# Two decoder layers in split fp32: attention turns, mixes and gates set in another order, output projections opened by half slabs

## The chip, the core and the metric

The kernel runs on one core of a Trainium2 chip. Its engines are TensorE (PE, matrix products; PEld is its weight load, which the profile lists apart), VectorE (DVE), ScalarE (ACT), GpSimd (POOL) and the DMA queues, here issued by SyncE (SP). The metric is the device time of one execution in microseconds, the median of several runs.

## The reference

One sequence of 256 positions, width 2048, passes two pre-norm layers and a final norm, all in fp32. Layer 0 is latent attention with 16 heads (rank 512 for queries and for keys and values, 128 plain and 64 rotary dimensions a head, values of 128). Layer 1 is attention in a sliding window of 128 with 32 query heads and 4 key and value heads of 64, a learned sink a head, and rotation of the first 16 dimensions.

```python
def reference(x, positions, layer_norm, mla_w_in, mla_q_norm, mla_w_uq, mla_kv_norm,
              mla_w_ukv, mla_w_out, swa_w_in, swa_sinks, swa_w_out, final_norm):
    for i in range(DEPTH):
        h = rmsnorm(x, layer_norm[i])
        j = i // N_MIXERS
        if i % N_MIXERS == 0:
            y, gate = mla_mixer(h, positions, mla_w_in[j], mla_q_norm[j], mla_w_uq[j],
                                mla_kv_norm[j], mla_w_ukv[j])
            w_out = mla_w_out[j]
        else:
            y, gate = swa_mixer(h, positions, swa_w_in[j], swa_sinks[j])
            w_out = swa_w_out[j]
        x = x + (y * jax.nn.silu(gate)) @ w_out
    return rmsnorm(x, final_norm)

def mla_mixer(h, positions, w_in, q_norm, w_uq, kv_norm, w_ukv):
    ...
    q = (rmsnorm(c_q, q_norm) @ w_uq).reshape(B, S, MLA_HEADS, MLA_NOPE + MLA_ROPE)
    q_nope = q[..., :MLA_NOPE]
    q_rope = rope(q[..., MLA_NOPE:], positions, MLA_ROPE)
    kv = (rmsnorm(c_kv, kv_norm) @ w_ukv).reshape(B, S, MLA_HEADS, MLA_NOPE + MLA_V)
    k_nope, v = kv[..., :MLA_NOPE], kv[..., MLA_NOPE:]
    k_rope = rope(k_rope[:, :, None, :], positions, MLA_ROPE)[:, :, 0, :]
    y = mla_causal_attention(q_nope, q_rope, k_nope, k_rope, v)
    return y, gate

def swa_sink_attention(q, k, v, sinks):
    ...
    m = jnp.maximum(jnp.max(s, axis=-1, keepdims=True), sink)
    e = jnp.exp(s - m)
    p = e / (jnp.sum(e, axis=-1, keepdims=True) + jnp.exp(sink - m))
    o = jnp.einsum('bnhgqk,bnkhd->bnqhgd', p.astype(v.dtype), vw)
    return o.reshape(B, S, SWA_WIDTH)
```

## The kernel before

Everything is kept transposed: the width lies on the 128 partitions in 16 chunks, the 256 positions along the free axis. An fp32 product is made of three float32r matmuls, high times high, high times low and low times high (`proj`, L250 to L252). `slab` does eight chunks of that: 24 matmuls of 128x256, half of the sum over the width, so two slabs make one chunk of a projection.

**Weights.** They stream once from memory. `Weights` holds a list of pieces of up to 128x1024 in the order in which `w.add` names them; SP's queue loads them as `wraw` (512 KB each), ACT casts the high part `whi` (L89) and DVE subtracts to get the low part `wlo` (L90), two pieces ahead of the one in use, and loads run three further ahead. So the order of `w.add` has to be the order of use, and with it goes the order of work on SP, ACT and DVE.

**Layer 0.** After the latent projections (`cq`, `ck`, in `lat`) a loop over eight groups g of two heads runs on TensorE: plain queries from `cq` (24 matmuls), the mix of the group before, rope parts of the queries (12), keys from `ck` (24), values (24, L520 to L522: here `ck` is the stationary side and the weights move), then four gate slabs from `hs` (96). After the first slab come the scores (16), and after the third the turn: six transposes (`turn`, L342 and L343) that bring the softmax rows `p` under the keys. ACT and DVE make of them the high part `pth`, the low part `ptl`, and for the second half of the queries a plain fp32 tile `pt1`. The mix multiplies values by them (L450 to L453); L453 is a plain fp32 product, which TensorE runs as two passes, the others are float32r. Its result is multiplied by the gate (`sg`) and split into `ys`. The last mix stands alone in front of the output projection, 16 chunks of two slabs from `ys` (`w_o0`).

**Layer 1.** Two chunks of keys (four slabs each two), the sum of squares `total` (L222, plain fp32) after the first of them, `rsqrt` (DVE and POOL) to `r1`, its row `r1B`, the rotated keys `k1s`; then values from four quarters of the weights (`sc<-whi,hs`, L603 to L605). A loop over 16 pairs of query heads c follows, in which every step is a half query slab, values and gate of pair c-1 (`values`, `gated`), the turn of pair c, the scores of pair c+1, the other half of a query two pairs ahead, and a whole gate chunk. `silu` (L361 to L363) reads the gate's PSUM bank as `hx`. The second output projection (`w_o1`) and the tail with the final norm end the program.

**What sets the order.** Each engine runs its instructions in one fixed order; the framework derives it from the order of the calls and from its own priorities, so places differ a little from the code. `ps_p` has three PSUM banks for projections, `ps_s` two for scores, `ps_t` one tile for turns, `ps_y` one bank for mixes and values. `pth`, `ptl` and the value tiles have one buffer each.

Of the kernel before, what the change touches and what calls it, by code (L numbers as in the profile page):

```python
# [25 lines left out]
P = 128  # L26
# [17 lines left out]
WARM = 2  # L44
MASK_MLA = [(i + 16) % 32 for i in range(32)]
# [54 lines left out]
def trunk(ctx: ExitStack, tc: tile.TileContext, a: dict):  # L100
# [11 lines left out]
    w = Weights(nc, wpool, raw_bufs=5, sub_bufs=4, ahead_load=3, ahead_split=2)  # L112
    w.add(a["w_c"][0], SUB, SUB // 2)
# [8 lines left out]
    for c in range(KC):  # L122
        w.add(a["w_o0"][c], D)
# [6 lines left out]
    for c in range(KC):  # L130
        if c + 2 < KC:
            w.add(a["w_q1"][c + 2], D)
        w.add(a["w_g1"][c], D)
    for c in range(KC):
        w.add(a["w_o1"][c], D)
# [125 lines left out]

    def bank(pool_, tag):
        return pool_.tile([P, 512], F32, tag=tag, name=tag)
# [72 lines left out]
    def turn(pair, both):  # L336
# [9 lines left out]
        hi = work.tile([P, 6 * P], F32R, tag="pth", name="pth", bufs=1)  # L346
        lo = work.tile([P, 6 * P], F32R, tag="ptl", name="ptl", bufs=1)
# [20 lines left out]
    lat = {n: [const.tile([P, 2, S], F32R, tag=f"lat{n}{c}", name=f"c{n}{c}") for c in range(RC)] for n in "qk"}  # L368
# [73 lines left out]
    def mix(g, vt, pt, sgs):  # L442

        (vh, vl, v1), (pth, ptl, pt1) = vt, pt
        yp = bank(ps_y, "yp")
        for j in range(2):
            v = slice(j * VD, (j + 1) * VD)
            n = slice(j * S, (j + 1) * S)
            o = yp[:, n]
            mm(o, lhsT=vh[:, v], rhs=pth[:, n], start=True, stop=False)  # L450
            mm(o, lhsT=vl[:, v], rhs=pth[:, n], start=False, stop=False)
            mm(o, lhsT=vh[:, v], rhs=ptl[:, n], start=False, stop=False)
            mm(o[:, P:], lhsT=v1[:, v], rhs=pt1[:, j * P:(j + 1) * P], start=False, stop=True)  # L453
# [6 lines left out]
    mixes = None  # L460
    for g in range(HEADS // 2):
# [10 lines left out]
        if mixes:  # L472
            mixes()
        ps = bank(ps_p, "pp")[:, 0:S]
        up(ps, *w.next(), lat["q"])
        qr = work.tile([P, S], F32, tag="ro3", name="ro3")
        rope(qr, ps, cos0, sin0, MASK_MLA)
        qs = work.tile([P, 2, S], F32R, tag="qs", name="qs")
        stack_pair(qs, qr)
        if g == 0:  # L480
            t = bank(ps_y, "yp")
            tot = [q.total(t[:, 4 * i:4 * i + 4]) for i, q in enumerate((sq_x, sq_c["q"], sq_c["k"]))]
            r0 = rsqrt("r0", tot[0], D)

            sqc = rsqrt("sqc", tot[1], RANK, r0)
            nsq = const.tile([P, 2], F32, name="nsq")
            dve.tensor_tensor(out=nsq, in0=sqc, in1=r0, op=ALU.mult)
            dve.tensor_scalar(out=nsq, in0=nsq, scalar1=-MLA_SCALE, scalar2=None, op0=ALU.mult)
            skc = rsqrt("skc", tot[2], RANK, r0)
            sk = const.tile([P, 2], F32, name="sk")  # L490
            dve.tensor_tensor(out=sk, in0=skc, in1=r0, op=ALU.mult)
            t = bank(ps_y, "yp")
            r0B = row("r0B", r0, t[:, 0:S])
            skB = row("skB", sk, t[:, S:])
            ps = bank(ps_s, "sc")[:, 0:S]
            mm(ps, lhsT=fold, rhs=krn, start=True, stop=True)
            kr = work.tile([P, S], F32, tag="ro3", name="ro3")
            rope(kr, ps, cos0, sin0, MASK_MLA)
            dve.tensor_tensor(out=kr, in0=kr, in1=r0B, op=ALU.mult)
            split(krs, kr)  # L500
# [31 lines left out]
        for step in range(4):  # L532
# [24 lines left out]
            if step == 2:  # L557
                pth, ptl, pt1 = turn(pair, False)
# [359 lines left out]
```

## Time and profile before

| | us |
|---|---|
| runs | 681.96, 682.65, 677.71 |
| median | 681.96 |
| profiled execution, its own time | 679.97 |
| its span, first to last instruction | 678.2 |

The span and the time of the same execution differ by 1.77 us. The granted clock of TensorE is 0.999 over the span. The profile gives for each engine the busy time, and by windows of the span the busy time and the number of instructions in them; the timeline lists instructions with start and duration, and with the wait before them where there was one. The duration of a matmul (some 276 ns) is longer than its distance to the next one, since they are pipelined: the distance of the starts is what counts.

### The profile page before, as it was taken

The page shows a single profiled execution, that of the slowest core. Times are in us where ns is not written, and L with a number is a line of the kernel's source. Part 1 is how long each engine was busy: PE and PEld are TensorE (multiplying, and loading weights), DVE is VectorE, ACT ScalarE, POOL GpSimd, SP SyncE. Part 2 cuts the span into 40 slices and gives each one's busy share as a digit, 9 for nine tenths or more (in the row PEclk, how much of TensorE's full clock was granted, in tenths as well). Part 3 has the DMA queues.
Part 4 walks back from the last instruction along what each step waited for, and adds up shares of the span by engine and source line. Part 5 has one row for each costly group of instructions (what it writes and reads, how often), then busy time and mean ns, then how long its engine had stood idle before and what let it go on. Part 6 is the DMA issues. An engine that isn't in the chain of part 4 may idle for free.

```text
span 678.2 us, 14573 instructions
## 1 busy us (share of the span) xinstructions
PE 666.0 (98%) x5732; PEld 662.6 (98%) x5732; DVE 529.0 (78%) x1079; ACT 429.8 (63%) x855; POOL 66.4 (10%) x72
## 2 busy tenths in 40 slices
PE   8999999999999999999999999999999999999995
PEld 8899999999999999999999999999999999999995
DVE  4897886787787686666667799899899899766664
ACT  6666756756666675444445588878878878644431
POOL 3634000000000000111120000000000000022220
PEclk9999999999999999999999999999999999999999
DMA  8665344544554545555554554554553544565513
GB/s 310 236 221 176 137 162 170 174 155 147 179 172 141 183 160 182 185 192 181 189 183 163 169 175 143 169 187 128 184 183 130 186 167 145 162 208 191 191 59 125
DMA packets 34197, 116.99 MB, mean 173 GB/s; under 512 B 4177, under 2 KB 4817, under 8 KB 34129
## 3 DMA queue, kind: packets, MB, share of 16 engines
q1 hardware_dynamic: 33840, 115.54, 50.4%
q8 instruction: 45, 0.74, 0.4%
q10 hardware_dynamic: 288, 0.52, 0.2%
q14 instruction: 24, 0.19, 0.1%
HBM read 113.95 MB, written 2.10 MB: 171 GB/s over the span
## 4 chain that ended last, share of the span: by engine, by line
PE 90%; DVE 3%; ACT 3%; issue 1%; POOL 1%; DMA 1%; SPq 0%; DVEq 0%; ACTq 0%; POOLq 0%
PE pp L251 24%; PE pp L252 24%; PE pp L250 24%; ACT whi L89 2%; PE pt L342 2%; DVE wlo L90 1%; PE pp L748 1%; PE pp L520 1%; PE pp L522 1%; PE pp L521 1%; PE yp L670 1%; DMA wraw<-in_w_c 1%; PE pt L343 1%; PE sc L642 1%; PE sc L605 1%
## 5 line engine op out<-in xcount | busy, mean ns | idle before, releaser
L90 DVE TENSOR_TENSOR wlo<-wraw,whi 128x1024 fp32r<-128x1024 f32 (+1 forms) x217 | 259.6, 1198 | 96.1 <-ACT whi L89 96.0
L89 ACT CAST whi<-wraw 128x1024 fp32r<-128x1024 f32 (+1 forms) x217 | 222.7, 1028 | 135.5 <-PE pp L251 110.0
L252 PE MATMUL pp<-hs,wlo 128*128 128x256 f32 x860 | 237.9, 277 | 1.4 <-DVE wlo L90 1.4
L250 PE MATMUL pp<-hs,whi 128*128 128x256 f32 x860 | 238.9, 278 | 0.0
L251 PE MATMUL pp<-hs,whi 128*128 128x256 f32 x860 | 238.0, 277 | 0.5 <-DVE hs L200 0.5
L252 PEld LDWEIGHTS pp<-hs,wlo 128*128 128x128 f32 x860 | 161.5, 188 | 1.6 <-DVE wlo L90 1.6
L251 PEld LDWEIGHTS pp<-hs,whi 128*128 128x128 f32 x860 | 161.5, 188 | 0.9 <-DVE hs L200 0.9
L250 PEld LDWEIGHTS pp<-hs,whi 128*128 128x128 f32 x860 | 161.7, 188 | 0.0
L250 PE MATMUL pp<-ys,whi 128*128 128x256 f32 x480 | 133.8, 279 | 0.0
L251 PE MATMUL pp<-ys,whi 128*128 128x256 f32 x480 | 133.7, 279 | 0.0
L252 PE MATMUL pp<-ys,wlo 128*128 128x256 f32 x480 | 133.7, 279 | 0.0
L216 POOL TENSOR_TENSOR sq_x<-sq_x,sq 128x256 f32<-128x256 f32 x43 | 53.3, 1240 | 574.1 <-ACT sq L215 336.4
L252 PEld LDWEIGHTS pp<-ys,wlo 128*128 128x128 f32 x480 | 91.1, 190 | 0.0
L251 PEld LDWEIGHTS pp<-ys,whi 128*128 128x128 f32 x480 | 90.2, 188 | 0.0
L250 PEld LDWEIGHTS pp<-ys,whi 128*128 128x128 f32 x480 | 90.0, 188 | 0.0
L328 ACT ACTIVATE p<-p,nm 128x128 f32<-128x128 f32 x96 | 42.7, 446 | 15.3 <-DVE nm L324 15.3
L194 ACT CAST ys<-yg 128x256 fp32r<-128x256 f32 x32 | 12.2, 405 | 29.4 <-DVE yg L684 27.7
L250 PE MATMUL pp<-cq,whi 128*128 128x256 f32 x96 | 27.3, 284 | 0.0
L200 DVE SCALAR_TENSOR_TENSOR hs<-x,gains,hs 128x256 fp32r<-128x256 f32 x32 | 24.9, 791 | 3.0 <-ACT hs L199 3.0
L252 PE MATMUL pp<-cq,wlo 128*128 128x256 f32 x96 | 26.7, 278 | 0.0
L251 PE MATMUL pp<-cq,whi 128*128 128x256 f32 x96 | 26.7, 278 | 0.0
L302 ACT CAST qs<-ro 64x256 fp32r<-64x256 f32 x48 | 19.2, 400 | 8.3 <-DVE ro L296 7.7
(253 smaller groups left out, 1149.4 us busy)
## 6 DMA issues: line engine op xcount, KB each, us to landing
wraw<-in_w_g SPq DMA_DIRECT2D x64, 512.0 KB, 3.5
wraw<-in_w_o SPq DMA_DIRECT2D x64, 512.0 KB, 3.7
wraw<-in_w_q SPq DMA_DIRECT2D x32, 512.0 KB, 4.1
wraw<-in_w_ukv SPq DMA_DIRECT2D x16, 512.0 KB, 3.4
wraw<-in_w_c SPq DMA_DIRECT2D x15, 512.0 KB, 6.9
wraw<-in_w_uq SPq DMA_DIRECT2D x8, 512.0 KB, 3.7
wraw<-in_w_uq SPq DMA_DIRECT2D x8, 256.0 KB, 2.6
wraw<-in_w_k SPq DMA_DIRECT2D x4, 512.0 KB, 4.3
```

The lines of the kernel that those rows point to most:

```text
L89: self.nc.scalar.copy(out=hi, in_=src)
L90: self.nc.vector.tensor_tensor(out=lo, in0=src, in1=hi.bitcast(F32), op=ALU.subtract)
L194: act.copy(out=dst[:, 0, :], in_=src)
L200: dve.scalar_tensor_tensor(out=dst[:, 1, :], in0=src, scalar=col, in1=dst[:, 0, :].bitcast(F32), op0=ALU.mult, op1=ALU.subtract)
L216: pool.tensor_tensor(out=self.acc, in0=self.acc, in1=t, op=ALU.add)
L250: mm(ps, lhsT=wh, rhs=rhs[:, 0, :], start=first, stop=False)
L251: mm(ps, lhsT=wh, rhs=rhs[:, 1, :], start=False, stop=False)
L252: mm(ps, lhsT=wl, rhs=rhs[:, 0, :], start=False, stop=last)
L302: act.copy(out=dst[r, j, :], in_=src[r, :])
L328: act.activation(out=p[:, cols], in_=p[:, cols], func=AF.Exp, scale=-1.0, bias=nm[:, c:c + 1], accum_out=sm[:, c:c + 1])
L342: nc.tensor.transpose(t[:, 0, j * S + i * P:j * S + (i + 1) * P], p[:, i * P:(i + 1) * P], ident)
L343: nc.tensor.transpose(t[:, 1, j * P:(j + 1) * P], p[:, 2 * P:3 * P], ident)
```

## The change

The number and the kind of the matmuls stay. What moves:

- **Layer 0, groups.** The turn of group g-1 stands behind the keys of group g, the rope parts behind the turn, then the values, and the mix of group g-1 behind the values, ahead of the first gate slab. Group 0 has no turn and no mix, and its rope parts stand ahead of the keys as before. `held` carries values, softmax rows and gates to the next group. The pieces of `w_uq` and `w_ukv` are listed in the new order of use.
- **`mix`.** Both products `vh` with `pth`, then the two fp32 products of `v1`, then the four that are left, float32r again.
- **`opened`.** Each output projection begins with chunks 0 and 1 at once: half slab of chunk 0, last turn, half slab of chunk 1, last mix (layer 1: last values and gate), then the two other halves. `out_weights` lists the pieces so.
- **Layer 1, start.** `total` and `r1` stand after all keys; the row, the rotation tables and the keys `k1s` after the first quarter of the values. The first scores stand after both first queries, and gate 0 whole behind them.
- **Layer 1, loop.** Step c has the half query, values and gate of c-1, turn c, scores c+1, the other half query, the second half of gate c and the first half of gate c+1.
- **Places in SBUF.** `vs` becomes one tile 64 bytes off its start, `pth` and `ptl` get 256 bytes more and in layer 1 begin 192 bytes later.

Functions `ranks`, `pair_scores` and `rope_parts` hold lines that were in the loop; their work is the same.

```diff
+OFF = 16
...
+    def out_weights(name):
+        for half in range(2):
+            for c in range(2):
+                w.add(a[name][c][:, half * SUB:(half + 1) * SUB], SUB)
+        for c in range(2, KC):
+            w.add(a[name][c], D)
...
-        w.add(a["w_uq"][g], 1536)
-        w.add(a["w_ukv"][g], 2048)
+        uq, ukv = a["w_uq"][g], a["w_ukv"][g]
+        keys, turns = (ukv[:, 0:1024], 1024), (uq[:, 1024:], 512)
+        for ap, n in [(uq[:, 0:1024], 1024)] + ([turns, keys] if g == 0 else [keys, turns]) + [(ukv[:, 1024:], 1024)]:
+            w.add(ap, n)
...
+        for g, half in ((c, 1), (c + 1, 0)):
+            if g > 0:
+                w.add(a["w_g1"][g][:, half * SUB:(half + 1) * SUB], SUB)
...
+    def opened(turns, mixes):
+        both = [bank(ps_p, "pp") for _ in range(2)]
+        slab(both[0], 0, ys)
+        turns()
+        slab(both[1], 0, ys)
+        mixes()
+        for ps in both:
+            slab(ps, 1, ys)
+        return both
...
-        hi = work.tile([P, 6 * P], F32R, tag="pth", name="pth", bufs=1)
-        lo = work.tile([P, 6 * P], F32R, tag="ptl", name="ptl", bufs=1)
+        at = 3 * OFF if both else 0
+        hi, lo = (work.tile([P, 6 * P + 4 * OFF], F32R, tag=n, name=n, bufs=1)[:, at:at + 6 * P] for n in ("pth", "ptl"))
...
-        for j in range(2):
-            v = slice(j * VD, (j + 1) * VD)
-            n = slice(j * S, (j + 1) * S)
-            o = yp[:, n]
-            mm(o, lhsT=vh[:, v], rhs=pth[:, n], start=True, stop=False)
-            mm(o, lhsT=vl[:, v], rhs=pth[:, n], start=False, stop=False)
-            mm(o, lhsT=vh[:, v], rhs=ptl[:, n], start=False, stop=False)
-            mm(o[:, P:], lhsT=v1[:, v], rhs=pt1[:, j * P:(j + 1) * P], start=False, stop=True)
+        vj, nj = [slice(j * VD, (j + 1) * VD) for j in range(2)], [slice(j * S, (j + 1) * S) for j in range(2)]
+        for j in range(2):
+            mm(yp[:, nj[j]], lhsT=vh[:, vj[j]], rhs=pth[:, nj[j]], start=j == 0, stop=False)
+        for j in range(2):
+            mm(yp[:, j * S + P:(j + 1) * S], lhsT=v1[:, vj[j]], rhs=pt1[:, j * P:(j + 1) * P], start=False, stop=False)
+        for j in range(2):
+            mm(yp[:, nj[j]], lhsT=vl[:, vj[j]], rhs=pth[:, nj[j]], start=False, stop=False)
+            mm(yp[:, nj[j]], lhsT=vh[:, vj[j]], rhs=ptl[:, nj[j]], start=False, stop=j == 1)
...
+        if held:
+            pt = turn(held[1], False)
+            rope_parts(qs)
...
+        if held:
+            mix(g - 1, held[0], pt, held[2])
...
-            if step == 2:
-                pth, ptl, pt1 = turn(pair, False)
-        mixes = partial(mix, g, (vh, vl, v1), (pth, ptl, pt1), sgs)
-    mixes()
+        held = (vh, vl, v1), pair, sgs
...
+    turned = []
+    both = opened(lambda: turned.append(turn(held[1], False)),
+                  lambda: mix(HEADS // 2 - 1, held[0], turned[0], held[2]))
     for c in range(KC):
-        ps = bank(ps_p, "pp")
-        for half in range(2):
-            slab(ps, half, ys)
+        if c < 2:
+            ps = both[c]
+        else:
+            ps = bank(ps_p, "pp")
+            for half in range(2):
+                slab(ps, half, ys)
...
-        if c == 0:
-            r1 = rsqrt("r1", sq_x1.total(bank(ps_y, "yp")[:, 0:4]), D)
...
+    r1 = rsqrt("r1", sq_x1.total(bank(ps_y, "yp")[:, 0:4]), D)
...
+    vsb = const.tile([P, RC * 2 * S], F32R, tag="latq", name="vs")
+    vs = [vsb[:, OFF + 2 * S * i:OFF + 2 * S * (i + 1)].rearrange("p (h a d) -> p h a d", h=KVH, a=2) for i in range(2)]
     vps = [bank(ps_s, "sc")[:, 0:S] for _ in range(2)]
     for q in range(4):
+        if q == 1:
+            r1B = row("r1B", r1, bank(ps_y, "yp")[:, 0:S])
...
+    scores(0)
+    for _ in range(2):
+        next(ends[0])
     for c in range(KC):
         if c + 2 < KC:
             q = query(c + 2)
             next(q)
-        elif c + 1 < KC:
-            next(ends[c])
         if c > 0:
             values(c - 1)
             gated(c - 1)
-        pt_of[c] = turn(p_of.pop(c), True)
         if c + 1 < KC:
+            pt_of[c] = turn(p_of.pop(c), True)
             scores(c + 1)
         if c + 2 < KC:
             next(q)
+        if 0 < c < KC - 1:
             next(ends[c])
-            next(ends[c])
-        elif c + 1 < KC:
-            next(ends[c])
+        if c + 1 < KC:
             next(ends[c + 1])
+        if c + 2 == KC:
             next(ends[c + 1])
+    def last_turn():
+        pt_of[KC - 1] = turn(p_of.pop(KC - 1), True)
+    def last_values():
+        values(KC - 1)
+        gated(KC - 1)
     sq_x2 = Squares("sq_x2")
+    both = opened(last_turn, last_values)
```

Three places in the engines' orders. First TensorE in a group of layer 0, at the mix (`yp` is its bank; `pt` the tile `pt1`, `v` the tile `v1`; `cq` the query latents, `hs` the layer's input). Before:

```order
L252 MATMUL pp<-cq_170,wlo 128x256
L450 MATMUL yp<-pth,vh 128x256
L451 MATMUL yp<-pth,vl 128x256
L452 MATMUL yp<-ptl,vh 128x256
L453 MATMUL yp<-pt_2587,v_2436 128x128
L450 MATMUL yp<-pth,vh 128x256
L451 MATMUL yp<-pth,vl 128x256
L452 MATMUL yp<-ptl,vh 128x256
L453 MATMUL yp<-pt_2587,v_2436 128x128
L250 MATMUL pp<-cq_167,whi 128x256
L251 MATMUL pp<-cq_167,whi 128x256
```

Now (the rows behind it are the first gate slab):

```order
L578 MATMUL pp<-whi,ck_171 128x256
L478 MATMUL yp<-pth,vh 128x256 x2
L480 MATMUL yp<-pt_2693,v_2433 128x128 x2
L482 MATMUL yp<-pth,vl 128x256
L483 MATMUL yp<-ptl,vh 128x256
L482 MATMUL yp<-pth,vl 128x256
L483 MATMUL yp<-ptl,vh 128x256
L266 MATMUL pp<-hs_135,whi 128x256
L267 MATMUL pp<-hs_135,whi 128x256
```

The mix moved from between queries and rope parts to between values and the gate slab, and the two fp32 rows from its ends into its middle.

Second TensorE at the first output projection (`ys`, the gated result, is the moving side). Before, the last mix behind the last gate slab:

```order
L252 MATMUL pp<-hs_150,wlo 128x256
L450 MATMUL yp<-pth,vh 128x256
L451 MATMUL yp<-pth,vl 128x256
L452 MATMUL yp<-ptl,vh 128x256
L453 MATMUL yp<-pt_3613,v_3462 128x128
L450 MATMUL yp<-pth,vh 128x256
L451 MATMUL yp<-pth,vl 128x256
L452 MATMUL yp<-ptl,vh 128x256
L453 MATMUL yp<-pt_3613,v_3462 128x128
L250 MATMUL pp<-ys_151,whi 128x256
L251 MATMUL pp<-ys_151,whi 128x256
```

Now the turn, with the slab of chunk 0 ahead of it and the slab of chunk 1 behind it:

```order
L268 MATMUL pp<-ys_158,wlo 128x256
L369 MATMUL pt<-ident,p 128x128 x2
L370 MATMUL pt<-ident,p 128x128
L369 MATMUL pt<-ident,p 128x128 x2
L370 MATMUL pt<-ident,p 128x128
L266 MATMUL pp<-ys_151,whi 128x256
L267 MATMUL pp<-ys_151,whi 128x256
L268 MATMUL pp<-ys_151,wlo 128x256
```

and the mix behind the slab of chunk 1:

```order
L268 MATMUL pp<-ys_158,wlo 128x256
L478 MATMUL yp<-pth,vh 128x256 x2
L480 MATMUL yp<-pt_3679,v_3459 128x128 x2
L482 MATMUL yp<-pth,vl 128x256
L483 MATMUL yp<-ptl,vh 128x256
L482 MATMUL yp<-pth,vl 128x256
L483 MATMUL yp<-ptl,vh 128x256
L266 MATMUL pp<-ys_159,whi 128x256
L267 MATMUL pp<-ys_159,whi 128x256
```

The last turn and the last mix moved into the projection, each behind a half slab.

Third DVE in a step of layer 1's loop, around the gate's `hx` (`ri` belongs to the softmax, `ro` and `qs` to the query's rotation, `wlo` to the weights, `sg` is the gate). Before:

```order
L295 TENSOR_TENSOR ro_6125<-ro_6125,sin1R 128x256
L655 RECIPROCAL ri<-es 128x4
L90 TENSOR_TENSOR wlo<-wraw,whi 128x1024
L296 TENSOR_TENSOR ro_6123<-ro_6124,ro_6125 128x256
L361 SCALAR_TENSOR_TENSOR hx<-pp,r1B 128x256
L303 TENSOR_TENSOR qs<-ro_6123,qs 64x256 x2
L90 TENSOR_TENSOR wlo<-wraw,whi 128x1024
L363 SCALAR_TENSOR_TENSOR sg<-th,hx 128x256
```

Now:

```order
L322 TENSOR_TENSOR ro_6152<-ro_6152,sin1R 128x256
L706 RECIPROCAL ri<-es 128x4
L388 SCALAR_TENSOR_TENSOR hx<-pp,r1B 128x256
L323 TENSOR_TENSOR ro_6150<-ro_6151,ro_6152 128x256
L91 TENSOR_TENSOR wlo<-wraw,whi 128x1024
L330 TENSOR_TENSOR qs<-ro_6150,qs 64x256 x2
L390 SCALAR_TENSOR_TENSOR sg<-th,hx 128x256
```

`hx` moved ahead of a `wlo` and of the last step of the rotation.

More of the change, by code (lines that the diff above doesn't have):

```diff
@@ L540, in trunk @@
                 for j in range(2):
[L541 to L553 removed]
+                    pair.append(pair_scores(j, nm, sm, qh, ql, qs, kk))
                 dve.reciprocal(out=ri, in_=sm)
@@ L685, in gated @@
         split(ys[c], yg)
+    ends = [gate(c) for c in range(KC)]
     for c in range(2):
```

132 lines of the change are left out of this document (66 added, 66 removed).

## The prediction

> **What bounds the kernel now.** I read the page first, for which engine sets the end.
>
> ```profile
> span 678.2 us, 14573 instructions
> PE 666.0 (98%) x5732; PEld 662.6 (98%) x5732; DVE 529.0 (78%) x1079; ACT 429.8 (63%) x855; POOL 66.4 (10%) x72
> PE 90%; DVE 3%; ACT 3%; issue 1%; POOL 1%; DMA 1%; SPq 0%; DVEq 0%; ACTq 0%; POOLq 0%
> ```
>
> TensorE multiplies and loads weights for 98% of the span, and 90% of the chain that ended last lies on it. The change neither adds nor removes a matmul, so it can gain in two ways only: by waits of TensorE that go, and by matmuls that follow each other faster. Whether there are two speeds, the view by windows says. Its columns are the window, its length, then busy time and instruction count of PE, PEld, DVE, ACT and POOL, the granted clock, the DMA share and GB/s.
>
> ```profile
> 590.00:660.00 70.00, 70.00 (x620) 70.00 (x619) 47.10 (x53) 30.52 (x39) 18.96 (x13) 1.00 0.50 166
> 262.00:342.00 80.00, 80.00 (x682) 80.00 (x681) 52.91 (x57) 39.39 (x56) 13.76 (x13) 1.00 0.54 184
> 400.00:580.00 180.00, 180.00 (x1591) 180.00 (x1590) 166.83 (x432) 144.27 (x337) 0.00 (x0) 1.00 0.49 164
> 257.90:354.00 96.10, 96.10 (x818) 96.10 (x817) 63.77 (x71) 47.10 (x68) 15.88 (x15) 1.00 0.55 184
> 354.60:360.00 5.40, 5.40 (x48) 5.40 (x48) 2.55 (x3) 1.58 (x2) 0.70 (x1) 1.00 0.58 189
> 372.00:382.50 10.50, 10.50 (x92) 10.50 (x91) 7.64 (x12) 5.28 (x7) 0.00 (x0) 1.00 0.60 213
> 186.40:194.40 8.00, 8.00 (x70) 8.00 (x70) 6.95 (x15) 4.98 (x8) 0.00 (x0) 1.00 0.43 130
> ```
>
> The first two rows are the two output projections: the same 128x256 matmuls, clock 1.00 in both. A matmul row lasts 0.276 us and the next starts some 0.113 later, so a window's count has about 0.276 / 0.113 = 2.4 from beyond its edges. Then 70.00 / 617.6 = 113.3 ns a matmul, and 80.00 / 679.6 = 117.7. I call these the quick and the slow beat; they differ by 4.4 ns. Layer 1's loop (third row) is quick: 180.00 / 1588.6 = 113.3. The next three rows are the first output projection with the first key slabs, the second key slabs, and the first two queries: 96.10 / 815.6 = 117.8, 5.40 / 45.6 = 118.4, 10.50 / 89.6 = 117.2, all slow. The last row lies in a group of layer 0, behind its mix: 8.00 / 67.6 = 118.3, slow too. The groups of instructions inside the first two windows, and of the values (line, engine, operation, tile, shape, count, then busy us and mean ns), show the same:
>
> ```profile
> L250 PE MATMUL pp<-ys,whi 128*128 128x256 f32 x197 | 54.4, 276 | 0.0
> L250 PE MATMUL pp<-ys,whi 128*128 128x256 f32 x228 | 64.1, 281 | 0.0
> L520 PE MATMUL pp<-whi,ck 128*128 128x256 f32 x64 | 18.1, 283 | 0.0
> ```
>
> What turns one beat into the other, the timeline shows at the seams (start, duration, what). First a turn (six transposes) before a gate slab, then the last mix before the output projection:
>
> ```profile
> 205.06 0.27 PE L343 MATMUL pt<-ident,p 128*128 128x128 f32 x1
> 205.09 0.37 PE L250 MATMUL pp<-hs,whi 128*128 128x256 f32 x1
> 205.30 0.28 PE L251 MATMUL pp<-hs,whi 128*128 128x256 f32 x1
> 205.42 0.28 PE L252 MATMUL pp<-hs,wlo 128*128 128x256 f32 x1
> 205.53 0.28 PE L250 MATMUL pp<-hs,whi 128*128 128x256 f32 x1
> ...
> 257.68 0.38 PE L453 MATMUL yp<-pt,v 128*128 128x128 f32 x2
> 257.81 0.36 PE L250 MATMUL pp<-ys,whi 128*128 128x256 f32 x1
> 258.01 0.28 PE L251 MATMUL pp<-ys,whi 128*128 128x256 f32 x1
> 258.13 0.28 PE L252 MATMUL pp<-ys,wlo 128*128 128x256 f32 x1
> 258.25 0.28 PE L250 MATMUL pp<-ys,whi 128*128 128x256 f32 x1
> ```
>
> After the turn the starts step by 0.21, 0.12 and then 0.11; after the mix by 0.20 and then 0.12, and that step stays for the 816 matmuls of the fourth window. In this trace every mix of layer 0 is left in the slow beat, and it ends with the plain-f32 product of L453; every turn entered quick is left quick. Inside one stretch of slabs the beat does not change unless TensorE stalls or other operands come.
>
> **The change, part by part.** Sums are made against the profiled execution, 679.97 us (span 678.2 and 1.77 around it); the median shown, 681.96, lies 2.0 above it and the lowest run 2.3 below, so the level itself is known to about 2.
>
> *First output projection and keys.* The last mix now ends with a float32r product, and two half slabs and the turn stand ahead of it. If it hands on a quick beat, the 816 and 46 matmuls gain 862 x 4.4 ns = 3.8 us; if not, 0. No row shows a slab behind such a mix. Nearest for it: the layer's own values (L520, always slow, 283 ns, the stationary side an activation as in the mix) are followed by a quick slab in six of the eight groups. Against it: after layer 1's last values, which end in float32r too, the slabs are slow until the next stall:
>
> ```profile
> 583.03 0.28 PE L672 MATMUL yp<-pth,vs 128*128 128x256 f32 x1
> 583.26 0.28 PE L250 MATMUL pp<-ys,whi 128*128 128x256 f32 x1
> 583.38 0.28 PE L251 MATMUL pp<-ys,whi 128*128 128x256 f32 x1
> 583.50 0.28 PE L252 MATMUL pp<-ys,wlo 128*128 128x256 f32 x1
> ```
>
> I take 3.8, since the slabs ahead of the mix and the turn are quick and the f32 product that broke every mix is no longer last. First queries: 90 x 4.4 = 0.4; in both kernels they follow layer 1's first values, so 0 to 0.4; with no row nearer to either end I take 0.2.
>
> *Groups of layer 0.* Now the mix makes 60 matmuls slow (rope parts 12, keys 24, values 24) up to the slab of 194.4. After, keys follow the query and rope parts follow the turn: both quick. The values stay slow by their own operands. Gain 36 x 4.4 = 0.16 us a group with a quick slab behind the mix; with a slow one, 24 come back: 0.05. Seven groups: 0.4 to 1.1; I take 1.1, the same answer as above.
>
> *Stalls.* Around the first scores of layer 1 TensorE waits:
>
> ```profile
> 382.60:391.70 9.10, 8.87 (x73) 8.28 (x71) 7.99 (x26) 6.95 (x18) 0.00 (x0) 1.00 0.42 130
> 581.50:584.00 2.50, 2.42 (x21) 2.23 (x21) 2.05 (x4) 1.67 (x3) 0.00 (x0) 1.00 0.67 210
> PEld yp L670 <- DVE ptl L349: 0.3, 1, 0.3
> ```
>
> The first window needs 70.6 x 0.1133 = 8.0 us and takes 9.1. Afterwards the second query stands ahead of the first scores, and gate 0 and a half query (72 matmuls, 8.2 us) between them and their turn; so the 1.1 goes. What is late next is nothing I find: the second scores wait for queries done 8 us before. At the last values the 18.6 matmuls need 2.1 and take 2.5: the turn stood too close. Half a projection (24 matmuls, 2.7 us) stands between turn and values now as before, but the last gate's work on DVE lies a half slab further back; I take 0.3 of the 0.4, with 0 to 0.4 for the range.
>
> *Values at the slabs' distance, offsets of pth and ptl.* Only start addresses move: 64 bytes for the values, 192 for the turned weights. The loop is quick already, so nothing to win there; about 34 slow matmuls at 583.3 could go, 34 x 4.4 = 0.15 us; I take 0.1. Price if it harms: rival C.
>
> *The norm r1 and row.* The total moves behind both key slabs, the row and the key rotation behind a quarter of the values.
>
> ```profile
> 354.54 0.16 DVE L229 TENSOR_SCALAR rs_e<-yp 128x2 f32<-128x2 f32 x1 [0.98 <-PE yp L222]
> 354.78 0.70 POOL L235 TENSOR_TENSOR r<-rs_e,mhalf 128x2 f32<-128x2 f32 x1 [3.45 <-DVE rs_e L229]
> ```
>
> From the total this chain takes some 1.2 us; the quarter ahead of the row is 24 matmuls, 2.7 us, and covers it. Uncovered it would cost 1.2 once. Behind it on POOL stands nothing until the second layer's squares. The scores come 3 quarters and two queries later. Cost 0.
>
> *DMAs and splits.* The same 512 KB and 256 KB pieces are issued on SP's queue in the new order; at 166 GB/s and a DMA share of 0.5, no row of TensorE waits for a piece after the start. Cost 0 while the split keeps two pieces ahead.
>
> *DVE in a group.* From the keys' end to the scores TensorE now has turn 0.66, rope parts 1.36, values 2.83, mix 1.1, slab 2.72: 8.7 us. DVE must by then have done two kf, kk, ptl, three wlo, the rotation and two qs.
>
> ```profile
> L90 DVE TENSOR_TENSOR wlo<-wraw,whi 128x1024 fp32r<-128x1024 f32 x207 | 252.7, 1222 | 89.8 <-ACT whi L89 89.7
> L303 DVE TENSOR_TENSOR qs<-ro,qs 64x256 fp32r<-64x256 f32 x48 | 20.2, 421 | 3.3 <-ACT qs L302 0.5
> L509 DVE TENSOR_TENSOR kf<-pp,skB 128x256 f32<-128x256 f32 x16 | 6.7, 418 | 0.0
> L511 DVE TENSOR_TENSOR kk<-kf,kk 128x512 fp32r<-128x512 f32 x8 | 5.5, 691 | 0.2
> L349 DVE TENSOR_TENSOR ptl<-pt,pth 128x512 fp32r<-128x512 f32 x8 | 5.5, 682 | 0.0
> ```
>
> That is 0.84 + 0.69 + 0.68 + 3 x 1.22 + about 1.7 (four at 0.42) + 0.84 = 8.4 us: it fits by 0.3, or more since neighbours overlap. Cost 0; if the cover is gone, 0.3 x 7 = 2.
>
> Sum: 3.8 + 0.2 + 1.1 + 1.1 + 0.3 + 0.1 = 6.6, so 679.97 - 6.6 = 673.4 us. (The Trainium skill, page "SBUF — State Buffer", section "SBUF: two separate sides", says that the port pair shared with GpSimd is the only contention and that PE, ACT and the dedicated pair of DVE "never wait on anyone". By it neither an address nor the order of operands could change the beat, and the sum would be the stalls alone, 1.4. The trace does show two beats at one clock, but not their cause.)
>
> **The rivals.** B, the mix hands on the slow beat as before: the 3.8 stays and the groups give 0.4: 679.97 - 0.2 - 0.4 - 1.1 - 0.3 - 0.1 = 677.9. For it: the slow slabs after 583.26. Against: the f32 product is gone from the end.
>
> C, the slow beat locks into layer 1, on the slower side. The values' odd distance there may be what throws the beat back to quick in every head; with equal distances a slow entry would stay. It would hold for the loop and the second projection, (1588.6 + 617.6) x 4.4 = 9.7 us: 673.4 + 9.7 = 683.1 with the first projection quick, 677.9 + 9.7 = 687.6 without. It decides at the first turn: slow behind the first queries and still slow in the next slab. Against: every turn in the trace that was entered quick was left so, and scores and stalls reset others.
>
> D, the beat hangs on neither order nor address, and only waits go: 679.97 - 1.4 = 678.6. This is also the case that the change does not do what it sets out to. Against it: both seams above repeat at every turn and every mix. (It is what the rule named above would give.)
>
> E, a new wait in layer 1's loop: gates are split over two heads, and a query takes the bank of a gate half a slab (2.7 us) after its end, so the gate's hx must be read by then.
>
> ```profile
> 447.93 1.19 DVE L90 TENSOR_TENSOR wlo<-wraw,whi 128x1024 fp32r<-128x1024 f32 x1
> 449.37 0.41 DVE L361 SCALAR_TENSOR_TENSOR hx<-pp,r1B 128x256 f32<-128x256 f32 x1
> ```
>
> In the new order hx stands ahead of that wlo; adding the rows' durations along it, hx is done some 0.5 us in time (an estimate). Behind the wlo it would be 1.19 - 0.5 = 0.7 late, thirteen times, 9 at most; since the order puts it ahead, 0.1 to 0.3 each is nearer, 1.3 to 4: 674.7 to 677.4. The row of hx shows no wait now, which speaks against it.
>
> **How the numbers follow.** Forecast A 0.45 (its own range 671 to 675), B 0.28, C 0.10 (half of it at 687.6), D 0.08, E 0.09. One per cent is 6.8 us, about what a measurement of this kernel can tell from no change. A's centre stands just at it: against the shown median the line is 675.1, against the profiled execution 673.2; I give A 0.55 for over 1%, 0.25, and 0.05 more for B or E with a level 2 lower: faster 0.30. Slower by over 1% is the half of C, 0.05. Within 1% is the rest, 0.65. The range leaves out C's 0.10 above and as much of A below: 670 to 682.
>
> **What would show it.** In the changed profile: a window of 90 us in the first output projection with 113.3 ns a matmul (A) or 117.7 (B); rope parts and keys at 276 ns, not 281; slabs behind a mix at 0.11 steps; no gap around the first scores (9.1 us for 73 rows now 8.2); L520's values still near 283; the loop at 12.9 us a head and no wait of TensorE on hx or qs. A loop above 13.2 a head would make it C or E, by whether the gaps are even or single.

## The result, and the profile after

| | us, median (range) | runs |
|---|---|---|
| before | 682.25 (677.71 to 682.65) | 4 |
| changed | 673.37 (672.84 to 675.75) | 4 |
| ratio | 0.9892, 95% interval 0.9843 to 0.9940 | |

Here and below a ratio leaves out the slow executions, those more than 1.5% above the lowest of their kernel.

The changed kernel is faster by about 1.1%, 673.37 us where 673.4 was forecast. Its profiled execution is the slowest of its four: 675.75, with a span of 674.0. So the two profiles differ by 4.2 us, half of what the medians differ by, and a good part of this section is about why.

The page after, the same lines as before:

```profile
span 674.0 us, 14601 instructions
PE 662.5 (98%) x5732; PEld 658.8 (98%) x5732; DVE 533.6 (79%) x1079; ACT 431.3 (64%) x855; POOL 63.7 (9%) x72
PE 91%; DVE 3%; ACT 2%; POOL 1%; DMA 1%; issue 1%; SPq 0%; DVEq 0%; ACTq 0%; POOLq 0%
```

TensorE is still the bound, with as many matmuls. The windows after (columns as before): first projection, second projection, layer 1's loop, and the first scores of layer 1.

```profile
263.50:353.00 89.50, 89.50 (x793) 89.50 (x791) 60.60 (x65) 46.17 (x66) 15.87 (x15) 1.00 0.59 190
581.50:661.50 80.00, 80.00 (x680) 79.88 (x679) 50.62 (x64) 32.83 (x43) 18.71 (x13) 1.00 0.45 145
400.00:560.00 160.00, 160.00 (x1415) 160.00 (x1415) 150.14 (x395) 128.53 (x303) 0.00 (x0) 1.00 0.49 161
376.00:385.10 9.10, 9.06 (x79) 8.85 (x79) 8.78 (x26) 7.09 (x18) 0.00 (x0) 1.00 0.35 116
```

Per matmul, with the 2.4 from beyond the edges taken off: 113.2 ns, 118.1, 113.3. The two projections have changed places: the first was slow and is quick, the second was quick and is slow. At the first scores 79 rows now fit where 73 did: 76.6 x 0.1133 = 8.7 us of work in 9.1, so 0.4 us is lost there instead of 1.1.

The groups of layer 0, by the timeline: the first row of a turn, five groups apart, after and then before.

```profile
113.34 0.38 PE L369 MATMUL pt<-ident,p 128*128 128x128 f32 x2
233.98 0.38 PE L369 MATMUL pt<-ident,p 128*128 128x128 f32 x2
```

```profile
106.92 0.38 PE L342 MATMUL pt<-ident,p 128*128 128x128 f32 x2
228.92 0.38 PE L342 MATMUL pt<-ident,p 128*128 128x128 f32 x2
```

120.64 / 5 = 24.13 us a group, 122.00 / 5 = 24.40 before. The values (L520 before, L577 and its neighbours now) run at 276 ns instead of 283:

```profile
L577 PE MATMUL pp<-wlo,ck 128*128 128x256 f32 x64 | 17.7, 276 | 0.0
L654 PE MATMUL sc<-whi,hs 128*128 128x256 f32 x32 | 9.1, 285 | 0.0
```

L654, layer 1's first values, is still slow. Last, the timeline around the opened mix, where a step decided that the prediction had not seen:

```profile
259.81 0.28 PE L483 MATMUL yp<-ptl,vh 128*128 128x256 f32 x1
259.92 0.28 PE L266 MATMUL pp<-ys,whi 128*128 128x256 f32 x1
260.04 0.28 PE L267 MATMUL pp<-ys,whi 128*128 128x256 f32 x1
260.16 0.28 PE L268 MATMUL pp<-ys,wlo 128*128 128x256 f32 x1
...
261.81 0.28 PE L267 MATMUL pp<-ys,whi 128*128 128x256 f32 x1
261.93 0.28 PE L268 MATMUL pp<-ys,wlo 128*128 128x256 f32 x1
262.05 0.45 PE L266 MATMUL pp<-ys,whi 128*128 128x256 f32 x2
262.45 0.38 PE L267 MATMUL pp<-ys,whi 128*128 128x256 f32 x1
...
263.03 0.28 PE L268 MATMUL pp<-ys,wlo 128*128 128x256 f32 x1
263.14 0.28 PE L267 MATMUL pp<-ys,whi 128*128 128x256 f32 x1
263.26 0.28 PE L268 MATMUL pp<-ys,wlo 128*128 128x256 f32 x1
PEld pp L267 <- DVE ys L211: 0.2, 1, 0.2
```

The opened mix is left in the slow beat after all (steps of 0.12 from 259.92 on). Two microseconds later TensorE waits for the last `ys`, which the mix has only just produced: three starts from 261.93 to 262.45 take 0.52 us where 0.35 is usual, and the weight loads lost 0.3 us in all. Behind that wait the steps become 0.11, and stay so for the whole projection.

The second projection has a wait at the same place, behind the last values, and there it goes the other way:

```profile
581.59 0.28 PE L266 MATMUL pp<-ys,whi 128*128 128x256 f32 x1
581.70 0.28 PE L267 MATMUL pp<-ys,whi 128*128 128x256 f32 x1
581.82 0.28 PE L268 MATMUL pp<-ys,wlo 128*128 128x256 f32 x1
582.02 0.50 PE L266 MATMUL pp<-ys,whi 128*128 128x256 f32 x2
582.36 0.28 PE L267 MATMUL pp<-ys,whi 128*128 128x256 f32 x1
582.48 0.28 PE L268 MATMUL pp<-ys,wlo 128*128 128x256 f32 x1
582.60 0.28 PE L267 MATMUL pp<-ys,whi 128*128 128x256 f32 x1
```

The steps are 0.11 ahead of it and 0.12 behind it: a wait of 0.2 us, and the slow beat of 118.1 ns starts there. So a wait can throw the beat either way.

The two profiles add up. First projection and keys -3.9 (862 matmuls), groups -1.9 (7 x 0.27), first scores -0.7, second projection +3.0 (677.6 matmuls x 4.4), new waits behind the mix and the last values +0.4, and -1.2 from the start, where nothing was changed (the row of the first norm begins at 66.08 after and 67.26 before; in the other profiles of this document it lies between 65.8 and 67.7). That is -4.3, against -4.2 between the spans; without the start it is -3.1.

### The profile page after: what moved, and what is told of

It is laid out like the page before. It is cut to its first block, busy times and chain, and to the rows that moved or that the text cites. A ratio compares the mean times of both kernels' runs of the same rounds, so it can differ in the third digit from the quotient of the medians.

```text
span 674.0 us, 14601 instructions
## 1 busy us (share of the span) xinstructions
PE 662.5 (98%) x5732; PEld 658.8 (98%) x5732; DVE 533.6 (79%) x1079; ACT 431.3 (64%) x855; POOL 63.7 (9%) x72
## 4 chain that ended last, share of the span: by engine, by line
PE 91%; DVE 3%; ACT 2%; POOL 1%; DMA 1%; issue 1%; SPq 0%; DVEq 0%; ACTq 0%; POOLq 0%
PE pp L267 25%; PE pp L266 25%; PE pp L268 24%; PE pt L369 2%; PE yp L721 1%; PE pp L806 1%; ACT whi L90 1%; PE pp L578 1%; PE pp L577 1%; PE pp L576 1%; DMA wraw<-in_w_c 1%; DVE wlo L91 1%; PE pt L370 1%; PE sc L693 1%; PE sc L654 1%
## 5 line engine op out<-in xcount | busy, mean ns | idle before, releaser
L232 POOL TENSOR_TENSOR sq_x<-sq_x,sq 128x256 f32<-128x256 f32 x43 | 50.7, 1179 | 567.0 <-ACT sq L231 334.9
L361 ACT ACTIVATE p<-p,ri 128x256 f32<-128x256 f32 x48 | 23.8, 496 | 0.0
```

Of the source, the lines that this page charges most:

```text
L232: pool.tensor_tensor(out=self.acc, in0=self.acc, in1=t, op=ALU.add)
L361: act.activation(out=p[:, P:], in_=p[:, P:], func=AF.Copy, scale=ri[:, 2 + j:3 + j])
```

## The experiments

The question after the result: does the order of the change make the beat quick, as its steps would have it, or do other things set the beat, which then stays? Every kernel was timed beside the kernel before; its times there moved from group to group of runs (medians 675.66, 679.57, 680.0 and 681.8; the last two, from the mix with its old end and a transpose on, were on other chips than the first two), so I compare where the times of a kernel lie and what its profile shows. A profile shows one execution, which need not be like the others of its kernel.

**What sits behind the last mix.** On the kernel before, six transposes behind the last mix.

```diff
     mixes()
+    t = ps_t.tile([P, 2, 512], F32, tag="pt", name="pt")
+    for i in range(6):
+        nc.tensor.transpose(t[:, i // 4, i % 4 * P:(i % 4 + 1) * P], ident, ident)
```

> The kernel before with one addition: six transposes of the identity, whose result nobody reads, between the last mix of layer 0 and the first output projection. Theory (the beat is a state that a seam sets and the matmuls behind it carry on): the projection and the keys run at 113.3 ns a matmul where the kernel before has 117.8, some 860 x 4.5 = 3.9 us gained, 0.7 us paid for the transposes, 3.2 us faster in all. Rival (the beat comes with the operands and their addresses): the projection stays at 117.8 and the kernel is 0.7 us slower. Rival (the beat is thrown anew in each execution): either, and not at the seam.

Measured 675.69 to 686.90, median 680.18, ratio 1.0056 (1.0031 to 1.0081). The profiled execution, 675.69, has the first projection quick, by its window:

```profile
258.00:348.00 90.00, 90.00 (x796) 90.00 (x796) 61.38 (x70) 46.63 (x67) 15.87 (x15) 1.00 0.58 188
```

90.00 / 793.6 = 113.4. So the beat is no matter of the operands of that projection. The gain was not in the median, though: the other nine lie at 679.34 and above, and no profile tells what was slow in them. Nor is the kernel before always as in its profile: in this group 13 of its 19 executions lie at 674.37 to 676.28, some 4 to 6 us below the profiled one. With one transpose in place of six:

> As the run with six transposes, with one alone. Theory in its strong form (any plain transpose between sets the quick beat): the projection at 113.3 ns, 3.7 us faster. Weaker form (the six of a turn are needed, or what counts is how the weight loads of several follow each other): 117.8 ns, no change. Rival of operands: 117.8 ns, 0.1 us slower.

Ten times in two bunches: 674.70 to 675.54 (five) and 682.06 to 685.61 (five). The profiled execution is of the second, 682.47, with two windows, the first projection and layer 1's loop:

```profile
250.00:340.00 90.00, 90.00 (x796) 90.00 (x795) 61.12 (x71) 48.43 (x74) 13.79 (x13) 1.00 0.58 187
400.00:580.00 180.00, 180.00 (x1535) 180.00 (x1534) 162.82 (x423) 141.14 (x329) 0.00 (x0) 1.00 0.49 156
```

The projection is quick (113.4), and the loop is slow from its first head to its last: 180.00 / 1532.6 = 117.4 ns, in a loop that was not touched. 1,533 matmuls at 4.1 more are 6.3 us in this window alone, and the bunches lie 7 apart. That is the lock-in of rival C of the prediction, seen on the kernel before with one instruction added; the turns in every head did not end it.

**The order inside the mix.** On the kernel before, `mix` alone as in the change (fp32 products in the middle):

```diff
-            mm(o, lhsT=vh[:, v], rhs=pth[:, n], start=True, stop=False)
...
-            mm(o[:, P:], lhsT=v1[:, v], rhs=pt1[:, j * P:(j + 1) * P], start=False, stop=True)
+        for j in range(2):
+            mm(yp[:, j * S + P:(j + 1) * S], lhsT=v1[:, vj[j]], rhs=pt1[:, j * P:(j + 1) * P], start=False, stop=False)
```

> The kernel before with the new order inside the mix alone (the fp32 products in the middle, a float32r product last). Theory: the slow stretch of 60 matmuls behind each of seven mixes shrinks to less than 10 (7 x 50 x 4.5 ns = 1.6 us), values included, and the first output projection with the keys is quick (3.8 us): 5 us faster, most of what the whole change gave. Rival (the values are slow by their operands): values stay at 117.8, 0.8 us less. Rival (the place of the mix in the group and the opened projection matter, not what it ends with): no change.

A miss: 678.89 to 681.99, ratio 1.0067 (1.0048 to 1.0087). The first projection stayed slow, and so did the 62 matmuls behind each mix:

```profile
256.80:352.90 96.10, 96.10 (x819) 96.10 (x817) 63.59 (x71) 47.02 (x69) 15.88 (x15) 1.00 0.57 183
```

96.10 / 816.6 = 117.7. TensorE waits inside this run's last mix too: from its first weight load to the first of its fp32 products 0.39 us pass (255.29 to 255.68), where the changed kernel takes 0.23 (258.67 to 258.90). The projection behind this wait of 0.16 us is slow. And the other way round, the changed kernel with the old order inside the mix:

> The changed kernel with the old order inside the mix (an fp32 product last), all else of the change kept. Theory: behind each mix the first gate slab is slow up to the scores (24 matmuls, 7 x 24 x 4.5 ns = 0.8 us), and the first output projection, the keys and the first queries are slow (3.9 us): 4 to 5 us slower than the changed kernel. Rival (the places count, not the order inside): as the changed kernel within 1 us.

A miss as well: 672.20 to 673.33, no slower than the changed kernel; the ratio is only 0.9959 (0.9945 to 0.9974), as the kernel before had its lowest median in this group. Groups and first projection are as quick as there (89.50 / 789.6 = 113.3), and in this execution the second projection too:

```profile
264.00:353.50 89.50, 89.50 (x792) 89.50 (x791) 60.77 (x65) 46.26 (x65) 15.91 (x15) 1.00 0.60 191
600.00:659.00 59.00, 59.00 (x523) 59.00 (x522) 38.47 (x48) 23.79 (x31) 14.63 (x10) 1.00 0.44 141
```

So the fp32 product at the end of the mix was not what set the slow beat. Where the mix stands matters: in front of `cq` (before, and with the mix alone changed) the slow beat stays for 60 matmuls, in front of the `hs` slab (changed, with either order) it is gone after 4 to 7.

**The changed kernel again.**

> The changed kernel once more, beside the kernel before on this chip. Theory (the beat of the long stretches is settled at seams where TensorE has waited, and a nanosecond there decides): groups of 24.13 us again, each with the same seams; the first projection quick again behind its wait; the second projection quick or slow, and the times in two clusters 3 us apart, 672.8 and 675.8. Rival (the beat comes with the program): second projection slow again, 116 to 118 ns a matmul in every execution, one cluster.

672.63 to 680.03, median 674.61, ratio 0.9939 (0.9905 to 0.9973): five times up to 673.5, four from 675.7 to 677.0, one at 680.03. The last is the profiled one, with both projections slow:

```profile
263.50:353.00 89.50, 89.50 (x763) 89.50 (x762) 59.22 (x64) 45.12 (x64) 16.04 (x15) 1.00 0.55 184
583.00:663.00 80.00, 80.00 (x681) 79.97 (x680) 51.66 (x63) 33.25 (x44) 18.70 (x13) 1.00 0.45 149
```

The same program held 793 rows in the first of these windows in its first profile, and 763 here: 113.2 and 117.7 ns. By the distances of all weight loads this execution has 943 more matmuls in the slow beat than that one, most of them in the first projection and the keys, and its time is 4.28 us longer: 4.5 ns each. The wait behind the mix was there in both, as long to 2 ns; once the projection behind it was quick, once it was not.

**Addresses.** The offsets at 0:

```diff
-OFF = 16
+OFF = 0
```

> The changed kernel with the offsets at 0, so that layer 1's values and turned weights start at the addresses that the layout gives. Theory (operands' distance does not set the beat): layer 1's loop quick at 12.91 us a head, the whole within 1 us of the changed kernel in the same cluster. Rival (the distance matters): the loop's values or the projection behind them in the slow beat, 3 us slower, or loop steps longer by 6 x 4.5 ns.

672.82 to 675.98, median 673.10: as the changed kernel. The profiled execution is the slowest of the eight, as that of the changed kernel was of its four; the other seven lie at 673.82 or below. Loop (first row) and second projection:

```profile
400.00:560.00 160.00, 160.00 (x1415) 160.00 (x1414) 150.11 (x395) 128.39 (x302) 0.00 (x0) 1.00 0.48 160
582.50:661.50 79.00, 79.00 (x673) 79.00 (x673) 50.09 (x63) 32.54 (x42) 18.66 (x13) 1.00 0.43 144
```

The loop has 1415 rows in 160 us with the offsets and without, and the second projection behind the values is slow in both profiles (117.8). This part of the change did nothing that can be seen.

**The wait behind the mix taken away.** Three chunks opened in each projection, so that a third half slab covers the chain from the mix to the last `ys`:

```diff
-        both = [bank(ps_p, "pp") for _ in range(2)]
+        both = [bank(ps_p, "pp") for _ in range(3)]
...
         mixes()
+        slab(both[2], 0, ys)
```

> The changed kernel with three chunks opened in each output projection: a third half slab stands behind the mix, so that TensorE no longer waits for the last gated result. Theory (in the changed kernel it was this wait that reset the slow beat which the last mix left): the waits of 0.3 us behind the mix go, the first projection stays slow for its 800 matmuls, 3.5 us lost, 0.3 won: 3 us slower than the changed kernel. Rival (the opened projection is quick by its order): 0.5 us faster than the changed kernel.

675.60 to 680.25, median 678.87, with a profiled execution of 677.40. First and second projection:

```profile
265.00:354.50 89.50, 89.50 (x762) 89.50 (x761) 59.47 (x64) 44.65 (x64) 15.81 (x15) 1.00 0.55 184
583.50:663.50 80.00, 80.00 (x709) 80.00 (x707) 53.00 (x67) 33.81 (x46) 18.95 (x13) 1.00 0.45 150
```

The waits are gone and the first projection is slow (117.8), as the theory has it. The second is quick (113.2), which it did not foresee: there the wait had gone with the slow beat. So between this profile and the first of the changed kernel one projection is exchanged for the other. In the times this kernel is the slower one, with ten executions at 675.60 or above where the changed kernel has five of ten at 673.48 or below; six of the ten lie at 678.64 or above, and no profile tells what else was slow in those. Three attempts to have the quick beat without the wait, first one transpose behind both last mixes:

> As the run with three chunks opened, with one transpose of the identity, whose result nobody reads, behind each of the two last mixes. Theory (one transpose sets the quick beat, as in the run with one transpose on the kernel before): both projections at 113.3 ns and no wait behind the mixes: 0.3 us faster than the changed kernel's fast cluster, 672.5 or so where that has 672.8, and no cluster 3 us above. Rival (the transpose did nothing there, it shifted a wait): as the run without it.

675.64 to 679.65; first projection slow (90.00 / 764.6 = 117.7). Then the mix with its old end, and one transpose or six behind it in layer 0:

> Three chunks opened, as in the run of that name, with the mix ending in an fp32 product again and, in layer 0, one transpose of the identity (nobody reads it) behind the last mix. Theory (an fp32 product directly followed by a transpose and a slab hands on the quick beat, as on the kernel before; a float32r product followed by one does not, as in the run with three chunks and a transpose): the first projection at 113.3 ns without any wait in it, 3.5 us faster than three chunks alone, lowest times near 672. Rival (what counts is chance at each seam, whatever stands there): first projection slow, 675.6 and up.

675.22 to 680.15, first projection slow, 117.7 again.

> As the run before it, with six transposes in place of one. Theory: first projection quick, 0.6 us longer than with one. Rival: slow, 676 and up.

676.25 to 680.93, slow. The theory that a transpose sets the quick beat falls: the quick beat went with it in both profiles on the kernel before and does not here. What holds is coarser: in the four kernels without a wait in the opened first projection, 40 executions lie at 675.2 or above.

**The first projection closed again**, with the rest of the change kept:

```diff
-    both = opened(lambda: turned.append(turn(held[1], False)),
-                  lambda: mix(HEADS // 2 - 1, held[0], turned[0], held[2]))
+            if step == 2 and g == HEADS // 2 - 1:
+                last_pt = turn(pair, False)
...
+    mix(HEADS // 2 - 1, held[0], last_pt, held[2])
```

> The changed kernel with the first output projection closed again: the last group's turn behind its third gate slab, the last mix ahead of the whole projection; layer 1 and the groups stay as changed. Theory (the mix hands the slow beat to slabs of ys, and only the wait behind the opened mix reset it): no wait in the projection, all of it slow, 3.5 us lost and 0.4 won; times at 675.5 and up, groups still 24.13. Rival (the opened order is what makes it quick): as three chunks or the changed kernel, 672.8. Rival (the mix ahead of a plain projection is settled anew each time): quick in some executions.

672.23 to 680.22, three of nine below 674.1. I had overlooked that TensorE then waits inside the mix, for `pt1`; the profile, chain of waits and window:

```profile
PEld yp L481 <- ACT pt L381: 0.3, 1, 0.3
256.00:352.00 96.00, 96.00 (x850) 96.00 (x849) 64.48 (x73) 49.11 (x69) 15.88 (x15) 1.00 0.57 190
```

With that wait the projection is quick (113.3), without being opened. So the opened order is not needed, and a wait ahead of it is what the quick first projections of the changed kernels have in common. It is not enough: inside the same mix the kernel before waits 0.05 us and the run with the mix alone 0.16, and both were slow. Whether the length of the wait decides was not tested. The theory's times of 675.5 and up were a miss.

**Both put together.** The first projection with two chunks, which keeps its wait, and the second with three, which loses its own:

```diff
+        if first == 3:
+            slab(both[2], 0, ys)
...
+    both = opened(last_turn, last_values, 3)
```

> The changed kernel with the first projection opened by two chunks as it is (its wait behind the mix stays) and the second by three (its wait behind the values goes). Theory (a wait of TensorE throws the beat over, most often to quick where it was slow, and to slow where it was quick; without a wait the beat is handed on): first projection quick in most executions, second quick in all; lowest times at 672.3, most of them below 673.5, a smaller cluster at 676 with the first projection slow, none with both slow, so none at 680. Rival (the second projection's beat is chance): a cluster 3 us above the lowest with the first projection quick and the second slow.

672.91, 672.95, 673.44, 673.63, 676.77, 676.91; ratio 0.9911 (0.9878 to 0.9944). Both projections of the profiled execution (672.95) are quick:

```profile
264.00:353.50 89.50, 89.50 (x793) 89.50 (x792) 60.44 (x65) 46.15 (x66) 15.87 (x15) 1.00 0.58 189
579.00:659.00 80.00, 80.00 (x709) 80.00 (x708) 53.00 (x67) 33.84 (x46) 18.95 (x13) 1.00 0.45 150
```

Two bunches as expected, and none at 680. This kernel differs from the one with three chunks in the first projection alone, where it has its wait back: four of its six executions lie at 673.63 or below, and none of that kernel's ten below 675.60 (on another chip). Six executions do not show it faster than the changed kernel (673.37 and 674.61); what is shown is that the second projection was quick in all five profiles of kernels that open it with three chunks.

## Why the prediction was right, and where it was wrong

The total came out to a tenth of a microsecond, and that is luck. The sum took 6.6 us off the profiled execution of the kernel before. Between the two profiled executions the gain is 4.2, of which 1.2 lies at the start and is not the change's; between the medians it is 8.9. The median of the kernel before alone moved between 675.66 and 682.25 from one group of runs to the next, and the repeated comparison shows less gain (ratio 0.9939) than the first (0.9892).

- **What bounds the kernel: right.** TensorE at two beats, 113 and 118 ns at one clock, and the beat of long stretches worth several microseconds. This carried the forecast.
- **First projection and keys, 3.8: right in size (3.9 in the profile), wrong in its reason.** The step said that the opened mix hands on a quick beat since slabs and turn ahead of it are quick and the fp32 product is no longer last. The mix handed on the slow one, the fp32 product is indifferent (the two runs on the mix), and the beat turned quick behind a wait. That wait was not in the sum at all: I gave no cost to the chain from the mix to the last two `ys`. It costs 0.3 us; in this execution some 3.5 went with it, in the profiled one of the repeat nothing. The size came out by another way than the one worked out.
- **First queries, 0.2:** 0; they stay slow behind L654.
- **Second projection, not in the sum:** quick before, so nothing was to be won; in the profile after it is slow from the wait at 582.02 on and costs 3.0. Rival C priced it, together with the loop; the forecast itself has no term for it.
- **Groups, 1.1: mis-sized, 1.9 in the profile.** The step that failed is "the values stay slow by their own operands". They were slow because they were entered slow; with the mix behind them they run at 276 ns with the same operands, so 60 matmuls a group gain and not 36. This is the steadiest part of the gain: from the second group on, a group takes 24.13 us in all ten profiles of kernels with the new order, and 24.39 to 24.41 in all four with the old one.
- **First scores, 1.1:** 0.7, as 0.4 is still lost there. **Last values, 0.3:** hardly any; the wait for `ptl` stayed (0.3 us), and the one behind it in the projection, 0.1 us before, is 0.2.
- **Offsets, 0.1:** nothing; the run without them shows no difference.
- **Two readings of the profile before** were not right. Not every turn entered quick is left so: the one of the first group, at 82.22, has gate matmuls in its middle and is entered in steps of 0.11 and left in steps of 0.12. And seven of the eight groups, not six, have a quick slab behind the values, which speaks a little more for the 3.8 than was said.
- **Rival B** (the mix hands on the slow beat) was what happened at the seam, without its price in four of the five profiles with the first projection opened by two chunks. **Rival C** did not come in the changed kernel, but the run with one transpose shows that the slow beat can lock into the loop, at about 7 us of the 9.7 it was priced at. Its reason falls: that run has the old places of values and turned weights, which were to throw the beat back to quick. **Rival E** did not come: the loop is at 113.3 ns and shows no wait on `hx`. **Rival D** falls by the groups, whose beat changed with the order in every profile; of the first projection it is half true, as its beat differs between executions of one program. By the Trainium skill ("SBUF — State Buffer", "SBUF: two separate sides") the port pair that DVE shares with GpSimd is the only one at which engines wait for each other, and TensorE never waits on anyone. No run here tests that: moving the operands by 64 and 192 bytes left the beat as it was, and what the other engines access was not varied. The cause of the two beats stays open.

How much of the gain is the change's own? The lowest of all executions of the kernel before is 674.34, of the changed kernel 672.63: 1.7 us with, it seems, every long stretch quick in both. The groups alone give 1.9. The rest of the 5 to 9 us between the medians would then be in how often the long stretches fall into the slow beat. That is not steady: in the group of runs where the kernel before was at 675.66, the changed kernel with the old mix was only 2.5 us below it. A part of it goes with waits at two or three places, as the runs with three chunks show; the rest is not explained.

**What stays open:** what in the chip makes the two beats, why a mix in front of `hs` recovers within 7 matmuls and one in front of `ys` or `cq` does not, why the same wait is followed by the quick beat in one execution and not in the next, and why a wait turns the beat quick in the first projection and slow in the second. No run here tells that. Nor was it tried to reset the beat behind L654, where some 200 slow matmuls are left in most profiles.

## What to carry to other kernels

Where an engine is busy without a gap, look at the distance from start to start, stretch by stretch, before looking for waits: 4.4 ns on a matmul was worth more here than the waits that the change took away. A stretch that is slow with certain operands is not slow because of them until it has been entered another way. And compare bunches of times, not two medians: here most kernels have times some 3 us apart, which is what the beat of one long stretch is worth. A profile of one execution says which stretch was slow in that execution, not in the kernel.

## What the runs showed of the hardware

- At a granted clock of 1.00, float32r matmuls of 128x256 follow each other at 113.2 to 113.4 ns or at 117.4 to 118.1 in the long windows above, none of them between. The slow beat held for some 1,500 matmuls on end, through transposes, scores and values (117.4 in the loop of the run with one transpose).
- One program takes either beat in the same stretch in different executions: 793 or 763 rows in the same 89.5 us.
- A wait of TensorE of 0.3 us ahead of the first projection was followed by the quick beat in five of the six profiles that have it; in the four kernels with three chunks, which have none there, the projection was slow in all four.
- A wait of 0.1 to 0.2 us ahead of the second projection was followed by the slow beat in the four profiles of changed kernels that have it, in three of which the beat had been quick just ahead; in the six without it the projection was quick. In the kernel before, where the beat just ahead was slow, a wait of 0.1 us there was followed by the quick beat.
